# The mixer of a conv/delta-rule layer: heads' Gram chains side by side, inverse in batches, output rows in another order, finer turns, and a planner with other durations

## The chip, the cores and the metric

The kernel runs on 1 core of one Trainium2 chip. The metric is the device time of one execution in microseconds (us); several executions are given by their median. Engines are named as in the profile: PE (TensorE matmul), PEld (its weight load), DVE (VectorE), ACT (ScalarE), POOL (GpSimd), SP (SyncE, which issues the DMAs).

## The reference

One layer on x of 2048 x 1024, float32. The mixer, which the change touches, computes

```python
h = adaln(x, ...)
p = h @ w_in[layer]
gate_b, gate_c, h_conv, q, k, v, z, a, bt = jnp.split(p, split_at, axis=-1)
ya = gate_b * causal_depthwise_conv(gate_c * h_conv, conv_w_mix[layer])
ya = rms_norm(ya.reshape(b, s, CONV_GROUPS, CONV_GROUP_DIM), ...)
qkv = jax.nn.silu(causal_depthwise_conv(jnp.concatenate([q, k, v], axis=-1), conv_w_qkv[layer]))
...
o = chunked_gated_delta_rule(q, k, v, g_dec, beta)
o = rms_norm(o, g_dn_out[layer]) * jax.nn.silu(z)
y = jnp.concatenate([ya, yb], axis=-1) @ w_out[layer]
x = x + gate_m[:, None, :] * y
```

with 4 heads of 128; the delta rule solves one unit lower triangular system per head and chunk (`tri = I + beta * k k^T * decay`) and carries a 128 x 128 state per head from chunk to chunk. A feed-forward part (gate/up and down projections) and a last norm follow; the change leaves their code alone.

## The kernel before, in words

**Stages.** The mixer goes over 4 blocks (`b`) of 512 tokens, each of CH = 4 chunks of 128. Every dense product is done in float32r with high and low halves, three matmuls of 128x512 for one; all of them are issued by `dmm` (L302 to L306; the profile puts them at L304). In a block the dense stream on PE is: strips of the projection for k, q, v (4 heads each, 24 matmuls a strip), 3 strips of z, then for m = 0..3 three strips of the convolution part (`gate_c`, `h_conv`, `gate_b`), the fourth strip of z, and the output projection: 2 halves n of 4 row groups kp, each 24 matmuls over 4 chunk tiles t. kp 0 and 1 read `ya` (the convolution half, tiles yah and yal), kp 2 and 3 read `yb` (the delta-rule half, tiles ym). Block 0 runs part of its first strips before the turn of the mixer proper.

**Side chains.** The rest is written as generators that `spawn` puts on a list. After each Q = 6 dense matmuls `tick` resumes each generator whose awaited tiles are ready by the planner's reckoning (`due`), or which counts down a number of ticks:
- `head_chain`: the gates a, b are turned (L832), a series of some 25 small POOL operations gives g (L836 to L870), a cumulative sum on PE (L874 to L876), then decay masks `E` (POOL L885, PE L890, ACT L893, POOL L894). Then for one head after another the Gram chain: k is transposed (L812), squares are summed (ACT L818), `kd` and M = k k^T * E * bk are made (DVE L903, L913, POOL L905, L914), the 32x32 diagonal blocks are masked out (POOL L918) and gathered (DVE L922). Then the inverse of all diagonal blocks: out to DRAM and in again in another layout (L932, L937), 31 elimination steps on DVE (L946, L948), out and in again (L954, L956), and the block diagonal matrices X by 32 POOL operations of 128x64 (L965).
- `q_chain` (L1038, L1039), `v_chain` (L1053); `level_chain`, two heads in each: X transposed on DVE (L982), the mask M of the level on POOL (L984), then products and updates on PE, ACT and DVE (L990 to L1025).
- `chunk_chain`: for each of the 4 chunks the three hops PE L1075/L1078, DVE L1080 to L1083 -> PE L1087, DVE L1091 -> PE L1095/L1097, DVE L1103/L1104; POOL L1082 decays the state.
- `out_chain` per chunk: sums of squares (ACT L1112), scales (POOL L1113 to L1117), waits for all 4 strips of z (`yield from wait("z", NH)`), transposes (PE L1123), DVE L1125, ACT L1129 and DVE L1130 make the `yb` tiles ym.
- `mix_chain` per m: squares, group sums on PE (L1196, L1197), root, reciprocal (DVE L1200), yah and yal (L1202, L1203).
- `transpose_split`: the next block's x is turned (PE L528) and split (ACT L533, DVE L534, L535); `second_norm` turns the finished rows of the block before for the next stage (ACT L505, L554, PE L559).

**What sets the order.** `Clock` notes each instruction as it is emitted, with a modelled begin and end from a table of durations (`COST` and the branches of `note`). From the strips of q on (`clock.pinned`) each engine's instructions, and the DMA issues of SP, are pinned in the order of their modelled begins; nothing may overtake. Weights come through `next_w`, three strips ahead, in the order of `requests`, split by ACT L371 (high) and DVE L373 (low). PSUM has 4 banks pd for the dense stream and 4 banks pm for the chains. `drain` empties the list of chains; it stands ahead of the last tile of kp 2, n = 0, and at the block's end.

## Time and profile before

| | |
|---|---|
| median of 3 runs | 2571.94 us (2569.77 to 2575.55) |
| the profiled execution's own time | 2577.32 us |
| its span, first to last instruction | 2575.3 us |
| mean granted TensorE clock | 0.972 |
| busy: PE, DVE, ACT, POOL | 2388.1, 1839.5, 1014.1, 678.0 us |
| mixer blocks 0, 1, 2, 3, roughly | 62 to 337, 337 to 638, 638 to 934, 934 to 1227 us |
| gate/up products, down products | 1227 to 2098, 2098 to 2575 us |

Matmuls overlap in the records, so one of 128x512 lasts about 0.39 us while they follow each other every 0.23 us; a wait shows as idle time before an instruction and what ended it (`[2.17 <-ACT ym L1129]`). The granted clock is 1.0 or 0.5 at any one time, and a view by windows shows its mean.

### The profile page before, as it was taken

Reading aid. Unit: us, or ns where it says so; the run is one execution under the profiler, and the core shown is the slowest. Engines: PE = TensorE matmul, PEld = TensorE weight load, DVE = VectorE, ACT = ScalarE, POOL = GpSimd, SP = SyncE. Lnnn points to the kernel's source line nnn. Section 1 sums busy time; section 2 is a strip of 40 time slices with the busy share of each in tenths; the row PEclk is TensorE's granted clock in tenths of the full one; section 3 lists DMA queues with packets and bytes.
Section 4 is the critical chain, followed back from the end, with each engine's and each line's share of the span. In section 5 each row is a group of like instructions: output and inputs, shape, how many; then the busy total and the mean of one; then the engine's idle time right before and its main releaser. Section 6 shows DMA issues by size and latency. Waiting matters only on the chain. (4 is left out here: it accounts for less than half of the span.)

```text
span 2575.3 us, 30876 instructions
## 1 busy us (share of the span) xinstructions
PE 2388.1 (93%) x11243; PEld 1956.8 (76%) x11243; DVE 1839.5 (71%) x2594; ACT 1014.1 (39%) x1764; POOL 678.0 (26%) x800
## 2 busy tenths in 40 slices
PE   6879988899899999899799999999999999999996
PEld 4768777787677777787578888878888877887774
DVE  6886659866696657777766565787565559878898
ACT  3533445234543446234643333533333323322332
POOL 2631256113642236212100000000000036434426
PEclk9999999999999999999899999999999999999998
DMA  7442345524452344324575333564333265333332
GB/s 235 115 103 66 115 139 172 142 70 133 150 143 66 111 135 116 94 59 150 171 221 177 94 115 109 165 201 142 92 115 109 87 216 180 111 117 125 126 133 114
DMA packets 397534, 336.98 MB, mean 131 GB/s; under 512 B 39475, under 2 KB 338748, under 8 KB 397382
## 3 DMA queue, kind: packets, MB, share of 16 engines
q1 hardware_dynamic: 397126, 334.91, 42.4%
q8 instruction: 88, 1.44, 0.2%
q14 instruction: 64, 0.52, 0.1%
q10 hardware_dynamic: 256, 0.10, 0.0%
HBM read 261.55 MB, written 73.41 MB: 130 GB/s over the span
## 5 line engine op out<-in xcount | busy, mean ns | idle before, releaser
L371 ACT CAST whi<-wraw 128x1024 fp32r<-128x1024 f32 x278 | 291.9, 1050 | 388.5 <-PE pd L304 192.8
L373 DVE TENSOR_TENSOR wlo<-wraw,whi 128x1024 fp32r<-128x1024 f32 x275 | 341.2, 1242 | 108.1 <-ACT whi L371 105.4
L304 PE MATMUL pd<-hTh,whi 128*128 128x512 f32 x896 | 367.0, 410 | 1.1 <-DVE hTh L534 1.1
L304 PE MATMUL pd<-hTl,whi 128*128 128x512 f32 x896 | 355.9, 397 | 1.1 <-DVE hTl L535 1.1
L304 PE MATMUL pd<-hTh,wlo 128*128 128x512 f32 x896 | 355.4, 397 | 0.0
L1478 POOL TENSOR_TENSOR wraw<-wraw 128x1024 f32<-128x1024 f32 x2 | 5.0, 2522 | 786.5 <-DMA wraw<-in_w_down_dram 786.5
L304 PEld LDWEIGHTS pd<-hTh,whi 128*128 128x128 f32 x896 | 172.7, 193 | 37.2 <-DVE hTh L534 2.6
L304 PEld LDWEIGHTS pd<-hTh,wlo 128*128 128x128 f32 x896 | 171.9, 192 | 37.2
L304 PEld LDWEIGHTS pd<-hTl,whi 128*128 128x128 f32 x896 | 172.2, 192 | 35.8 <-DVE hTl L535 2.2
L1672 DVE TENSOR_TENSOR acc<-acc,pd 128x512 f32<-128x512 f32 x192 | 127.9, 679 | 29.6 <-PE pd L304 28.7
L1432 DVE TENSOR_TENSOR sg<-sg,pd 128x512 f32<-128x512 f32 x44 | 30.2, 687 | 165.6 <-PE pd L304 157.7
L1555 ACT CAST xh<-ra 128x640 fp32r<-128x640 f32 (+1 forms) x88 | 62.6, 719 | 197.8 <-PE pm L304 162.4
L1164 DVE SCALAR_TENSOR_TENSOR cv<-cb,pcb,cv 128x512 f32<-128x512 f32 x144 | 130.2, 904 | 4.6
L1564 POOL TENSOR_TENSOR xl<-ra,xh 128x640 fp32r<-128x640 f32 (+1 forms) x40 | 67.2, 1680 | 159.1 <-ACT xh L1555 154.8
L304 PE MATMUL pd<-whi,ym 128*128 128x512 f32 x256 | 93.7, 430 | 11.9 <-ACT ym L1129 11.9
L1672 DVE TENSOR_TENSOR acc<-acc,pm 128x512 f32<-128x512 f32 x120 | 81.6, 681 | 18.1 <-PE pm L304 17.6
L1272 POOL TENSOR_TENSOR cv<-cv 128x512 f32<-128x512 f32 x32 | 46.6, 1464 | 137.7 <-DVE cv L1271 93.2
L1601 POOL TENSOR_TENSOR wraw<-wraw 128x512 f32<-128x512 f32 x40 | 69.8, 1765 | 44.2 <-DMA wraw<-in_w_down_dram 44.2
L1082 POOL TENSOR_TENSOR state<-state,eg 128x512 f32<-128x512 f32 x15 | 21.2, 1411 | 225.8 <-PE pm L1078 225.7
L1200 DVE RECIPROCAL cv<-cv 128x512 f32<-128x512 f32 x16 | 53.7, 3353 | 35.6 <-ACT cv L1199 35.6
L965 POOL TENSOR_TENSOR X<-Dg,ck 128x64 f32<-128x64 f32 x128 | 40.0, 351 | 144.0 <-DMA Dg<-dx 144.0
L304 PE MATMUL pd<-S2h,whi 128*128 128x512 f32 x176 | 69.6, 395 | 7.3 <-ACT whi L371 7.3
(455 smaller groups left out, 6499.7 us busy)
## 6 DMA issues: line engine op xcount, KB each, us to landing
wraw<-in_w_in_dram SPq DMA_DIRECT2D x112, 512.0 KB, 4.4
wraw<-in_w_gate_up_dram SPq DMA_DIRECT2D x88, 512.0 KB, 3.9
ra<-act SPq DMA_DIRECT2D x80, 448.0 KB, 4.1
act<-S SPq DMA_DIRECT2D x80, 256.0 KB, 2.3
act<-act SPq DMA_DIRECT2D x68, 256.0 KB, 2.2
wraw<-in_w_ada_dram SPq DMA_DIRECT2D x32, 512.0 KB, 3.9
wraw<-in_w_out_dram SPq DMA_DIRECT2D x32, 512.0 KB, 3.7
wraw<-in_w_down_dram SPq DMA_DIRECT2D x22, 512.0 KB, 3.5
```

The costliest lines, as they stand in the source:

```text
L304: mm(*args, **kw)
L371: nc.scalar.copy(hi, raw)
L373: (lo_engines.popleft() if lo_engines else nc.vector).tensor_sub(lo, raw, hi.bitcast(F32))
L965: nc.gpsimd.tensor_mul(Xv[:, e, j], xc[:, e, h * CH + j].unsqueeze(1).to_broadcast([P, NBASE, HB]), bmb)
L1164: nc.vector.scalar_tensor_tensor(cv, cb[:, t:t + BLK], tap[t], cv, op0=ALU.mult, op1=ALU.add)
L1200: nc.vector.reciprocal(sy, sy)
L1272: nc.gpsimd.tensor_add(xr, xr, yo)
L1432: nc.vector.tensor_add(s5[i], s5[i], a[i])
L1555: nc.scalar.copy(hi, raw[:, c0:c1, :])
L1564: eng.tensor_sub(lo, raw, hi.bitcast(F32))
L1601: nc.gpsimd.tensor_mul(r[:, hs], r[:, hs], gate_f[:, hs])
L1672: nc.vector.tensor_add(accs[s, u][:, ns], accs[s, u][:, ns], ps)
```

## The change

- **Planner.** Other durations: POOL operations cost 0.14 us and 1.7 ns an element, and 0.42 or 0.6 us more while DVE is busy by the plan; a hand-over between engines 0.2 us (was 0.15); on one engine 0.1 us (0.14 on POOL, 0 on PE), where nothing was charged. A chain may ask `due` for two free pm banks (`yield 2, ...`), and one of lower standing for one more.
- **Turns.** In the mixer `tick` runs after each 3 dense matmuls; head, diagonal, level, chunk and out chains are asked first.
- **Gram chains.** Masking and gathering of the diagonal blocks and the level's mask M (before: in `level_chain`) go into a `diagonal_chain` per head, so that the next head's Gram product need not wait for it.
- **Inverse.** The elimination steps are emitted four at a time, each batch by a time of the plan. X is made by 8 operations of 128x256, those of heads 2 and 3 on DVE.
- **Dense order.** All 4 strips of z come before the convolution part. The output's row groups run kp 0, 2, 3, 1 in each half. `drain` ahead of the last tile of kp 2 stays in the last block alone.

```diff
+KPS = 0, 2, 3, 1
...
+    AGAIN = {"EngineType.PE": 0.0, "EngineType.Pool": 0.14}
...
-                cost = 0.2 + n * 2.0e-3
+                cost = 0.14 + n * 1.7e-3 + (0.42 if n < 200 else 0.6) * self.busy("EngineType.DVE", start)
...
+    FIRST_CHAINS = "head_chain", "diagonal_chain", "level_chain", "chunk_chain", "out_chain"
+
     def spawn(gen, delay=1):
-        side.append([gen, delay])
+        side.append([gen, delay, gen.__name__ not in FIRST_CHAINS])
+        side.sort(key=lambda e: e[2])
...
-    def due(w):
-        return max([clock.next_free("pm"), *(clock.ready(t) for t in w)]) + 0.3
+    def due(w, low):
+        banks, w = (w[0], w[1:]) if isinstance(w[0], int) else (1, w)
+        return max([clock.next_free("pm", banks + low), *(clock.ready(t) for t in w)]) + 0.3
...
-        if count[0] % Q == 0:
+        if count[0] % (Q // 2 if mixing[0] else Q) == 0:
...
-                    yield kT[:, h, :],
+                    yield 2, kT[:, h, :]
...
-                    yield from take("lv", 1)
-                    md = lv_tile([P, CH, NBASE, BASE])
...
                     done["kk"] += 1
-                    yield md,
-                    nc.vector.tensor_reduce(Dg[:, h], md.rearrange("p j b c -> p j c b"), op=ALU.add, axis=AX.X)
-                    give("lv", 1)
+                    spawn(diagonal_chain(M, Dg[:, h]), 1)
                 nc.gpsimd.tensor_mul(sk, sk, nk)
                 done["sk"] = True
-                yield 1
+                yield from wait("dg", NH)
...
-                    if k % 2:
-                        yield mxq,
+                    if k % 4 == 1:
+                        yield clock.ready(mxq, True) - 1.5
...
-                    for j in range(CH):
-                        for e in range(2):
-                            nc.gpsimd.tensor_mul(Xv[:, e, j], xc[:, e, h * CH + j].unsqueeze(1).to_broadcast([P, NBASE, HB]), bmb)
+                    for e in range(2):
+                        (nc.vector if h > 1 else nc.gpsimd).tensor_mul(
+                            Xv[:, e], xc[:, e, h * CH:(h + 1) * CH].unsqueeze(2).to_broadcast([P, CH, NBASE, HB]), by_base(HB))
...
+            def diagonal_chain(M, dst):
+                yield from take("lv", 1)
+                md = lv_tile([P, CH, NBASE, BASE])
+                nc.gpsimd.tensor_mul(md, M.rearrange("p j (b c) -> p j b c", c=BASE), by_base(BASE))
+                yield md,
+                nc.vector.tensor_reduce(dst, md.rearrange("p j b c -> p j c b"), op=ALU.add, axis=AX.X)
+                give("lv", 1)
+                mm_ = ap_.tile([P, CH, P], F32, name="ym", bufs=8)
+                nc.gpsimd.tensor_mul(mm_, M, bm(lmask[LEVELS[0]], CH))
+                Mms.append(mm_)
+                done["dg"] += 1
...
-            for h in range(NH - 1):
-                z_strip(h)
...
-            z_strip(NH - 1)
...
-                for kp in range(4):
+                for kp in KPS:
...
                         if n == 0 and kp == 2 and t == CH - 1:
-                            drain()
                             if b + 1 < NB:
                                 spawn(transpose_split(xblock(b + 1), Gm, Sm, *hT), 1)
                             else:
+                                drain()
                                 clock.pinned = mixing[0] = False
...
-                            dmm(pso[t], yl, wh[:, k, :], start=False, stop=(kp == 3 and k == 1))
+                            dmm(pso[t], yl, wh[:, k, :], start=False, stop=(kp == KPS[-1] and k == 1))
```

What this does to the order is shown at three places of block 1 (the changed kernel's lines are 6 to 13 higher for the same code: L914 becomes L920, L1123 becomes L1135).

POOL, the Gram chains of the first heads (sk, ym, lv: scale, M and masked M of a head; nq, rq: of q; ss: the finished rows' norm), before:

```order
L905 TENSOR_TENSOR sk_2769<-nk_2767,mhalf_86 128x4
L914 TENSOR_TENSOR ym_3214<-ym_3214,bk_2770 128x512
L918 TENSOR_TENSOR lv_3217<-ym_3214,ck_80 128x512
L1040 TENSOR_SCALAR nq_2768<-nq_2768 128x4
L1041 TENSOR_TENSOR rq_2771<-nq_2768,mhalf_86 128x4
L1042 TENSOR_SCALAR rq_2771<-rq_2771 128x4
L499 TENSOR_SCALAR ss_3176<-ss_3176 128x1
L500 TENSOR_TENSOR ss_3176<-ss_3176,mhalf_86 128x1
L905 TENSOR_TENSOR sk_2769<-nk_2767,mhalf_86 128x4
L914 TENSOR_TENSOR ym_3333<-ym_3333,bk_2770 128x512
L918 TENSOR_TENSOR lv_3336<-ym_3333,ck_80 128x512
```

And now:

```order
L911 TENSOR_TENSOR sk_2745<-nk_2743,mhalf_86 128x4
L920 TENSOR_TENSOR ym_3269<-ym_3269,bk_2746 128x512
L911 TENSOR_TENSOR sk_2745<-nk_2743,mhalf_86 128x4
L920 TENSOR_TENSOR ym_3294<-ym_3294,bk_2746 128x512
L1047 TENSOR_TENSOR lv_3297<-ym_3269,ck_80 128x512
L1047 TENSOR_TENSOR lv_3302<-ym_3294,ck_80 128x512
L911 TENSOR_TENSOR sk_2745<-nk_2743,mhalf_86 128x4
L505 TENSOR_SCALAR ss_3187<-ss_3187 128x1
L506 TENSOR_TENSOR ss_3187<-ss_3187,mhalf_86 128x1
L920 TENSOR_TENSOR ym_3332<-ym_3332,bk_2746 128x512
L911 TENSOR_TENSOR sk_2745<-nk_2743,mhalf_86 128x4
L924 TENSOR_TENSOR sk_2745<-sk_2745,nk_2743 128x16
```

Two heads' M stand side by side, their masks (now L1047) follow, and the operations on q (L1040 to L1042 before) are behind all four heads.

DVE, the end of the inverse (yal: the matrices in elimination; X: the block diagonal ones; cb, cv: convolution part; wlo: low halves of weights), before:

```order
L948 TENSOR_TENSOR yal<-yal,lv 128x16
L1220 TENSOR_TENSOR cb<-pd,cv 128x512
L1222 COPY uhalo_2759<-cb 128x2
L1225 TENSOR_SCALAR cv<-cb,pcb 128x512
L1227 SCALAR_TENSOR_TENSOR cv<-cb,pcb,cv 128x512 x2
L373 TENSOR_TENSOR wlo<-wraw,whi 128x1024
L438 SCALAR_TENSOR_TENSOR wraw<-wraw,cs 128x1024
L1219 COPY cb<-uhalo_512 128x2
L1231 TENSOR_TENSOR cv<-cv,pd 128x512
L982 STREAM_TRANSPOSE lv<-X 128x512
```

And now:

```order
L948 TENSOR_TENSOR yal<-yal,lv 128x16
L1241 TENSOR_TENSOR cv<-cv,pd 128x512
L380 TENSOR_TENSOR wlo<-wraw,whi 128x1024
L1203 TENSOR_TENSOR lv<-cv,lv 128x512
L380 TENSOR_TENSOR wlo<-wraw,whi 128x1024
L1210 RECIPROCAL cv<-cv 128x512
L463 TENSOR_TENSOR Sf<-pd,pca 128x8
L1211 SCALAR_TENSOR_TENSOR cv<-cv,pcb 128x512
L963 TENSOR_TENSOR X<-Dg,ck 128x256 x2
L1213 TENSOR_TENSOR yal<-cv,yah 128x512
L963 TENSOR_TENSOR X<-Dg,ck 128x256 x2
L981 STREAM_TRANSPOSE lv<-X 128x512 x4
```

Between the last elimination step and the transposes of X stand now the first mix chain's subtraction, reciprocal and product (L1193, L1200, L1201 before), which stood behind the transposes; the convolution's L1220 to L1227 of the first m went ahead of the last steps.

PE, the last chunk's products and the turning of its output (kd, E, ch: chunk chain; ck,ch: the transposes of `out_chain`; ym and yah: output projection; hT: projection), before:

```order
L1095 MATMUL pm<-ch,kd 128x128 x4
L1097 MATMUL pm<-ch,E 128x128 x4
L1123 MATMUL pm<-ck,ch 128x128 x4
L304 MATMUL pd<-whi,ym 128x512
L304 MATMUL pd<-wlo,ym 128x512
```

And now the turning of the last chunk's output (the products L1107 and L1109 of that chunk are 39 dense matmuls ahead of it):

```order
L311 MATMUL pd<-hTh,wlo 128x512
L1135 MATMUL pm<-ck,ch 128x128 x4
L311 MATMUL pd<-hTh,whi 128x512
L311 MATMUL pd<-hTl,whi 128x512
L311 MATMUL pd<-hTh,wlo 128x512
L311 MATMUL pd<-whi,yah 128x512
L311 MATMUL pd<-wlo,yah 128x512
```

The last chunk was worked among matmuls that read ym; now its output is turned while the projection still runs.

The places of the steps on PE, as the number of dense matmuls of the block that stand ahead of them (counted in the order; 864 in a block, `yb` is read from number 720 on before and from 696 on now; in block 0 the count starts 60 matmuls into the block, so there 660 and 636):

| step | block 0 | block 1 | block 2 | block 3 |
|---|---|---|---|---|
| L832, before -> now | 12 -> 6 | 30 -> 36 | 30 -> 36 | 30 -> 36 |
| L874 (g) | 60 -> 51 | 96 -> 114 | 96 -> 114 | 90 -> 114 |
| L911, four heads | 96, 138, 180, 204 -> 120, 141, 165, 192 | 138, 174, 216, 246 -> 177, 180, 192, 195 | 138, 174, 216, 246 -> 177, 180, 192, 195 | 144, 180, 210, 234 -> 189, 198, 207, 225 |
| L990 (X needed) | 372 -> 429 | 492 -> 528 | 432, 444 -> 489 | 414, 432 -> 444 |
| L1075 of the last chunk | 660 -> 537 | 720 -> 609 | 720 -> 600 | 720 -> 537 |
| L1123, last | 678 -> 585 | 738 -> 669 | 738 -> 663 | 749 -> 597 |
| L528, first (next block's x) | 690 -> 660 | 750 -> 720 | 750 -> 720 | - |

More of the change, by code (lines that the diff above doesn't have):

```diff
@@ L77, in fit, with busy @@
         return s + cost
+    def busy(self, name, t):
+        return not any(a <= t < b for a, b in self.gaps[name])
     @staticmethod
@@ L91, in ready @@
         a, b, c, d = self.box(ap)
-        return max([0.0] + [t + (0.15 if x != eng else 0.0) for (e, f, g, h), w, t, x in self.touched[ap.name]
+        return max([0.0] + [t + (0.2 if x != eng else self.AGAIN.get(eng, 0.1)) for (e, f, g, h), w, t, x in self.touched[ap.name]
                             if (w or write) and a < f and e < b and c < h and g < d])
@@ L114, in place, with next_free @@
         return self.free_at[tensor.name]
-    def next_free(self, name):
+    def next_free(self, name, n):
         tag = next((t for t in self.slots if t.startswith(name + "_")), None)
         row = [x for x in self.slots[tag] if x not in self.kept] if tag else []
-        return self.used[row[0]] if len(row) >= 4 else 0.0
-    def next_free(self, name):
-        tag = next((t for t in self.slots if t.startswith(name + "_")), None)
-        row = self.slots[tag] if tag else []
-        return self.used[row[-4]] if len(row) >= 4 else 0.0
+        return max(self.used[x] for x in row[:n]) if len(row) >= 4 else 0.0
     def note(self, i):
@@ L138, in note @@
             begin = self.fit(eng, start, 0.45) - 0.45
-            end = self.fit("DMA", begin + 1.0, cost) + 0.6
+            end = self.fit("DMA", begin + 1.2, cost) + 0.8
             self.order(eng, begin, i)
@@ L285, in tick @@
                 go = e[1] <= 0
+            elif isinstance(e[1], float):
+                go = e[1] <= clock.pe
             else:
-                go = due(e[1]) <= clock.pe
+                go = due(e[1], e[2]) <= clock.pe
             if go:
@@ L294, in tick @@
                     ran = True
-        times = [due(e[1]) for e in side if not isinstance(e[1], int)]
+        times = [e[1] if isinstance(e[1], float) else due(e[1], e[2]) for e in side if not isinstance(e[1], int)]
         if must and not ran and times:
@@ L388, in requests @@
             for c0 in (2048, 1536, 2560, 3072):
-                for h in range(NH - (c0 == 3072)):
+                for h in range(NH):
                     yield col_strip, w_in, c0 + h * P
@@ L445, in settled @@
         yield
-        while clock.pinned and due(tiles) > clock.pe:
+        while clock.pinned and due(tiles, 0) > clock.pe:
             yield
@@ L1001, in level_chain @@
                 T, Y = {}, {}
-                yield tuple(Xs[h] for h in hs)
+                yield 2, *(Xs[h] for h in hs)
                 yield from take("lv", len(hs))
@@ L1239, in layer_kernel @@
                 pso = [dense_ps() for _ in range(CH)]
-                for kp in range(4):
+                for kp in KPS:
                     wh, wl = next_w()
```

39 lines of the change are left out of this document (18 added, 21 removed).

## The prediction

> **What bounds the kernel now.** The windows by stage came first: the stretch of the four mixer blocks, one block of it, and the first 73 us behind the mixer.
>
> ```profile
> core 0: us, PE busy (x) PEld busy (x) DVE busy (x) ACT busy (x) POOL busy (x), PEclk, DMA share, GB/s
> 62.00:1227.00 1165.00, 1062.29 (x5510) 878.80 (x5508) 845.25 (x1304) 503.42 (x1017) 423.40 (x601) 0.96 0.40 116
> 337.00:638.00 301.00, 272.98 (x1436) 225.93 (x1435) 220.78 (x337) 128.15 (x256) 111.91 (x156) 0.95 0.44 131
> 1227.00:1300.00 73.00, 58.72 (x250) 45.24 (x249) 47.18 (x63) 47.00 (x69) 8.14 (x11) 0.88 0.56 173
> ```
>
> PE is the busiest engine, yet it stands idle for 1165.0 - 1062.3 = 102.7 us of the mixer, and its granted clock there is 0.96 and not 1. DVE, next, is busy for 220.8 of block 1's 301 us, so the block is not DVE's as a whole. What can be won is PE's idle time and its lost clock. PE's own waits in the mixer say for whom:
>
> ```profile
> PE pm L874 <- POOL g L863: 26.3, 4, 7.8
> PE pm L990 <- DVE lv L982: 18.1, 4, 5.9
> PE pd L304 <- ACT ym L1129: 11.9, 6, 2.2
> PE pm L559 <- ACT wraw L554: 11.2, 8, 2.8
> PE pm L812 <- ACT cv L1165: 8.8, 7, 2.0
> PE pm L1123 <- POOL ch L1117: 8.3, 4, 3.1
> PE pm L1197 <- DVE lv L1193: 6.1, 1, 6.1
> PE pm L479 <- DVE E L1039: 4.5, 1, 4.5
> PE pm L1196 <- ACT lv L1192: 1.8, 1, 1.8
> ```
>
> Columns are total us, times, longest. These nine hold 97.0 of the 102.7 us. I call them A (the gate g, 26.3), B (the inverse: 18.1, and the 6.1 and 1.8 of a mix chain whose DVE step stands behind the inverse's, 26.0 together), C (the last outputs, 11.9 + 8.3 = 20.2), and the rest: L559, L812 and L479. The chain that ended last covers only the kernel's tail and says nothing here. The price of a matmul's place in the stream is that chain's row of six:
>
> ```profile
> 2352.01 1.36 PE pm L304 x6
> ```
>
> so 0.2267 us each. How many stand between two steps comes from the order; how long a step takes, from the trace.
>
> **A, the gate.** PE in block 1, and POOL, where the chain from L832 to L874 runs:
>
> ```profile
> 349.77 0.42 PE L832 MATMUL pm<-ck,cv 16*128 16x16 f32 x4
> 373.06 0.61 PE L874 MATMUL pm<-g,ck 128*128 128x16 f32 x2 [6.27 <-POOL g L863]
> ...
> 359.95 0.96 POOL L848 TENSOR_SCALAR sp_s<-sp_e 128x16 f32<-128x16 f32 x1 [3.73 <-ACT sp_e L845]
> 368.40 1.08 POOL L856 TENSOR_TENSOR sp_p<-sp_p,sp_z 128x16 f32<-128x16 f32 x1
> 369.90 0.22 POOL L856 TENSOR_TENSOR sp_p<-sp_p,sp_z 128x16 f32<-128x16 f32 x1
> ```
>
> The chain takes 23 us, 10 of them until ACT's exponential and 13 on POOL; the change takes nothing out of it. What covers it changes: 66 dense matmuls stood between, 78 stand now in blocks 1 and 2 (12 x 0.2267 = 2.7 us each), 78 for 60 in block 3 (4.1), 45 for 48 in block 0 (-0.7). Sum: -8.8 us, and 17.5 of the 26.3 stay. Bounds: one more copy stands ahead of the exponential on ACT, and POOL's 13 us hang on what else runs (one operation takes 1.08 us or 0.22, the two rows of L856); I take the count, and 3 us either way as an estimate.
>
> **B, the inverse.** POOL, DVE and PE in block 1:
>
> ```profile
> 489.96 9.79 POOL L965 TENSOR_TENSOR X<-Dg,ck 128x64 f32<-128x64 f32 x31 [0.97 <-DMA Dg<-dx]
> ...
> 491.80 0.71 DVE L982 STREAM_TRANSPOSE lv<-X 128x512 f32<-128x512 f32 x1 [4.32 <-POOL X L965]
> 501.39 0.65 DVE L1193 TENSOR_TENSOR lv<-cv,lv 128x512 fp32r<-128x512 f32 x1
> ...
> 502.09 0.79 PE L1197 MATMUL pm<-lv,gones_r 128*128 128x512 f32 x1 [6.12 <-DVE lv L1193]
> ```
>
> X takes 9.8 us on POOL after its data has landed; DVE waits for it, and a mix chain's L1193 stands behind in DVE's queue, for which PE waits in turn. Now X is 8 operations of 128x256, four on POOL, four on DVE. No row has that shape: on POOL it lies between 0.32 (9.79 / 31) and 1.47 (the page's L984, 128x512),
>
> ```profile
> L984 POOL TENSOR_TENSOR ym<-ym,ck 128x512 f32<-128x512 f32 x16 | 23.0, 1468 | 0.2
> ```
>
> by size 0.81, so four take 3.2 us; on DVE under 0.71 (L982, 128x512), by size 0.36, four 1.4. X is then ready 6.6 us sooner. The two rows of L856 show that a POOL operation can take 0.22 us or 1.08. [...] Against the sum speaks the order on DVE: the elimination ends one convolution step later than before (L1220 to L1227, and now L1231, stand around it). But L990 too stands later on PE, by 57, 36, 45 or 57, and 30 matmuls, 6.8 us or more, where B's waits were 26.0 / 4 = 6.5 us a block, and L1193 now stands ahead of X. I leave 1.5 us a block: -20. Bounds: -26, and -10 if half the shift is eaten by the later end.
>
> **C, the last outputs.** PE in block 1, then the first square and the last scaling of the next block's x on ACT:
>
> ```profile
> 596.07 0.60 PE L1123 MATMUL pm<-ck,ch 128*128 128x128 f32 x4
> 598.84 0.50 PE L304 MATMUL pd<-whi,ym 128*128 128x512 f32 x1 [2.17 <-ACT ym L1129]
> 605.38 0.79 PE L304 MATMUL pd<-whi,ym 128*128 128x512 f32 x1 [1.49 <-ACT ym L1129]
> ...
> 593.54 1.06 ACT L505 ACTIVATE ht<-kq 128x1024 bf16<-128x1024 f32 x1 [2.86 <-DMA kq<-in_x_dram]
> 605.23 2.18 ACT L521 ACTIVATE kq<-kq,ss 128x1024 f32<-128x1024 f32 x2
> ```
>
> Here the turned output is needed 6 matmuls after it is turned. With all z strips ahead of the convolution part the chains need not stop after chunk 1: the last L1123 stands at 585, 669, 663 and 597, the first `yb` matmul at 696 (636 in block 0). The shortest cover is 27 matmuls, 6.1 us, for a chain of 2.8 us (596.07 to 598.84). kp 0 ahead, kp 1 last cover the last mix chains. The next block's x can load once the last chunk has read k and q, over 100 matmuls (23 us) ahead of its turning, where the chain from 593.54 to 607.41 takes 14. So all of C goes: -20.2.
>
> **The rest.** L479's one wait, in block 0, is for what DVE does around L1039; it now stands ahead of the first L1038 and 24 matmuls farther on: -2 (0 to -4.5). L559 and L812 wait for ACT and DVE work that is not shortened: 0 (-10 to +10). Moving the level's mask to the diagonal chains, the finer turns (switches between the two kinds of matmul go from 372 to 386, by the order) and DVE's 1.4 us of X: covered by idle POOL and DVE, within the term for new waits below.
>
> **The clock.** Windows on three waits of A, B and C:
>
> ```profile
> 373.00:377.00 4.00, 3.94 (x12) 3.43 (x13) 0.65 (x3) 1.72 (x4) 3.85 (x7) 0.50 0.02 7
> 502.00:507.00 5.00, 4.91 (x16) 4.24 (x17) 4.89 (x9) 0.69 (x1) 0.00 (x0) 0.50 0.39 104
> 600.00:609.00 9.00, 6.38 (x17) 4.25 (x17) 1.44 (x2) 6.91 (x11) 4.67 (x10) 0.50 0.00 1
> ```
>
> After each kind of wait PE runs at half clock. The mixer loses 0.04 x 1165 = 46.6 us so; in these windows PE works 15.2 of 18 us, so 39 us cost matmuls. Of A, B and C (72.5 us) 23.5 stay, 68% go: 27 us; since a short wait can cost a whole half-clock stretch, I take -22 (-12 to -27).
>
> **Behind the mixer** PE waits for the feed-forward's first sums:
>
> ```profile
> PE pd L304 <- ACT whi L371: 7.3, 1, 7.3
> PE pd L304 <- ACT A11h L574: 3.4, 1, 3.4
> PE pd L304 <- DVE A11l L575: 0.9, 1, 0.9
> ```
>
> They start at the last tile of kp 2, now 24 matmuls earlier: -5.4 of 11.6 (0 to -8).
>
> **New waits.** All four chunks now run beside the convolution part; 24 of their hops (two chunks, three hops, four blocks) are new there. A hop's DVE step can stand behind another operation:
>
> ```profile
> L373 DVE TENSOR_TENSOR wlo<-wraw,whi 128x1024 fp32r<-128x1024 f32 x275 | 341.2, 1242 | 108.1 <-ACT whi L371 105.4
> PE pm L1087 <- DVE ch L1081: 0.4, 1, 0.4
> ```
>
> The chunks already there waited 0.4 us in all (second row), one L373 in front costs 1.24: 0 to +30, I take half a microsecond a hop, +12.
>
> **Sum**: -8.8 - 20 - 20.2 - 2 - 22 - 5.4 + 12 = -66. The profiled execution's own time of 2577.3 becomes 2511; the median of the runs lies 5.4 below it, at 2571.9, so 2506.
>
> **The rivals.**
> 1. DVE becomes the bound of the stretch behind the inverse.
>
> ```profile
> 500.00:613.00 113.00, 106.01 (x624) 90.44 (x625) 74.82 (x94) 44.32 (x91) 22.53 (x36) 0.92 0.28 84
> 390.00:490.00 100.00, 91.29 (x465) 75.74 (x464) 92.94 (x175) 41.67 (x106) 39.01 (x40) 1.00 0.58 162
> ...
> L535 DVE TENSOR_TENSOR hTl<-ht,hTh 128x512 fp32r<-128x512 f32 x32 | 32.8, 1027 | 1.0
> ```
>
> DVE has 75 us of work in block 1's stretch, and gets 7 more pairs of L534 and L535 (7 x 1.03 for the second, 10 for both as an estimate), less three L373 (3.7): 81. PE's own work in the new stretch is 240 x 0.2267 = 54, and some 220 small matmuls of the chains at 0.11 to 0.15 (L1123's four in 0.60): 79 to 87. At 93% (DVE's share from 390 to 490 us, second row) 81 takes 87.5, up to 8.5 us a block more than PE: +34, 2540. For it: those loads; against it: DVE was idle for a third of this stretch.
> 2. The inverse's end moves as far as L990 does. B and its part of the clock (26/72.5 of 22) stay: +28, 2534. For it: the elimination is emitted in longer batches and still stands among the same L373; against it: X's 6.6 us.
> 3. Slower: the serial chunk chain among DVE's long operations. 47 hops (16 chunks; block 0's first chunk has two), each behind one L373 and one operation like L1193 (0.65) would cost 47 x 1.89 = 89 against gains of 78: +11, 2583. It decides from 78 / 47 = 1.7 us a hop. Against it: the 0.4 us above.
> 4. Short waits cost no clock. If half clock follows only single waits of several microseconds, as in A and B, then C (28% of the 39 us, 11) gives back nothing there, and the clock term is 22/27 of that, 9, smaller: 2515. The window at 600 us speaks against it: its waits are 2.2 us or less, its clock 0.50. [...]
>
> **How the numbers follow.** Chances: the forecast 0.58, rival 1 0.15, rival 2 0.12, rival 3 0.09, rival 4 0.06. The likeliest's own range takes all of B (-6), L479 (-2.5), no new wait (-12), more clock (-5), more behind the mixer (-2.6) and half of the rest's -10: 2506 - 33 = 2473; I go on to 2465 for the whole -10 with A's 3. Upward B -10 (+10), new waits +30 (+18), clock -12 (+10), nothing behind the mixer (+5.4): 2549, which takes in rivals 1, 2 and 4; 2552 with A's 3. Left out is rival 3. A measurement of this kernel tells apart about 0.2%, 5 us. Faster: 0.58 + 0.15 + 0.12 + 0.06, less 0.03 for cases between rivals 1 and 3: 0.88; within 0.2% 0.03; slower 0.09.
>
> **What would show it.** A: L874's waits at 17 to 18 us. B: L990, L1196 and L1197 under 7 together, POOL's L963 near 0.8 each. C: no wait for L1129's counterpart. The clock of the mixer's window at 0.98. Rival 1 shows as dense matmuls and chains that wait for DVE while DVE has no idle time; rival 2 as L981 behind L963 late on DVE; rival 3 as waits of L1087's and L1095's counterparts of over 1.7 us. The prediction is wrong if the mixer doesn't get some 60 us shorter, or if the time changes outside it.

## The result and the profile after

The changed kernel takes 2485.57 us (median of 4 runs, 2484.74 to 2487.72) where the kernel before takes 2571.98 (4 runs, 2569.77 to 2575.55): a ratio of 0.9664, 95% interval 0.9647 to 0.9681, or 86.4 us less. The forecast was 2506, its range 2465 to 2552. The profiled execution of the changed kernel has an own time of 2487.72 and a span of 2485.9 us, 89.6 and 89.4 less than the profiled execution before.

First the stages. The two windows are the mixer (from block 0's first L838, L832 before, to the first up product of the feed-forward) and the first 76 us behind it:

```profile
core 0: us, PE busy (x) PEld busy (x) DVE busy (x) ACT busy (x) POOL busy (x), PEclk, DMA share, GB/s
62.20:1146.80 1084.60, 1033.28 (x5488) 859.54 (x5488) 851.38 (x1335) 518.10 (x1032) 391.86 (x489) 0.98 0.43 124
1146.80:1222.80 76.00, 70.82 (x314) 57.70 (x313) 45.17 (x60) 46.38 (x64) 7.52 (x11) 0.96 0.60 187
```

The same mixer before, from its first L832 to its first up product, took 1158.7 us, with PE busy for 1055.99. So it is 74.1 us shorter: PE idle fell from 102.7 to 51.3 (-51.4), and PE's busy time, from 1056.0 to 1033.3 (-22.7). That is the clock, 0.96 then and 0.98 now: the window even holds 6 dense matmuls more, since L838 stands 6 places earlier in block 0 than L832 did. Of the other 15.3 us of the span 12.2 lie behind the mixer (1351.3 to 1339.1), most of it in the first 76 us, where PE's idle time was 14.3 and is 5.2. The last 3.1 lie ahead of it (65.3 to 62.2): 1.4 of them are those 6 matmuls, which now count as the mixer's, and the rest I take for scatter, since the runs below have 62.0 to 65.5 there.

PE's waits (total us, times, longest) answer to those shown of before:

```profile
PE pm L880 <- POOL g L869: 20.1, 4, 8.6
PE pd L311 <- ACT whi L378: 4.9, 2, 4.7
PE pd L311 <- DVE cv L1280: 4.8, 3, 2.5
PE pm L818 <- DVE E L1036: 4.6, 2, 4.1
PE pm L565 <- ACT wraw L560: 3.6, 1, 3.6
PE pm L896 <- POOL lv L891: 2.9, 2, 1.5
PE pm L818 <- DVE cb L1169: 2.6, 2, 2.4
PE pm L1135 <- POOL ch L1129: 2.2, 4, 0.9
PE pm L485 <- DVE wraw L480: 2.0, 1, 2.0
PE pm L1099 <- DVE ch L1093: 1.1, 2, 0.5
PE pm L987 <- DVE lv L981: 0.7, 1, 0.7
PE pm L1107 <- DVE ch L1103: 0.7, 1, 0.7
```

A (L880) fell only from 26.3 to 20.1. B's three rows are down to L987's 0.7; L1206 and L1207 wait for nobody. Of C's two rows one is left, L1135, with 2.2. The chunks' hops, L1099 and L1107, wait 1.8 us in all.

### The profile page after: what moved, and what is told of

The parts are those of the page before. It is cut to its first block, busy times and chain, and to the rows that moved or that the text cites. A ratio compares the mean times of both kernels' runs of the same rounds, so it can differ in the third digit from the quotient of the medians.

```text
span 2485.9 us, 30764 instructions
## 1 busy us (share of the span) xinstructions
PE 2356.5 (95%) x11243; PEld 1937.9 (78%) x11243; DVE 1833.5 (74%) x2610; ACT 1024.0 (41%) x1771; POOL 644.7 (26%) x688
## 5 line engine op out<-in xcount | busy, mean ns | idle before, releaser
L380 DVE TENSOR_TENSOR wlo<-wraw,whi 128x1024 fp32r<-128x1024 f32 x275 | 346.4, 1260 | 98.0 <-ACT whi L378 91.3
L1176 DVE SCALAR_TENSOR_TENSOR cv<-cb,pcb,cv 128x512 f32<-128x512 f32 x144 | 136.4, 947 | 3.7
L1681 DVE TENSOR_TENSOR acc<-acc,pm 128x512 f32<-128x512 f32 x120 | 81.5, 679 | 17.2 <-PE pm L311 16.8
L311 PE MATMUL pd<-whi,ym 128*128 128x512 f32 x256 | 86.5, 398 | 0.0
L311 PE MATMUL pd<-A22h,whi 128*128 128x512 f32 x176 | 69.1, 392 | 4.6 <-DVE sg L1441 4.6
L311 PE MATMUL pm<-S4h,whi 128*128 128x512 f32 x176 | 69.2, 393 | 2.7 <-ACT sg L1435 2.7
L311 PE MATMUL pd<-S2h,wlo 128*128 128x512 f32 x176 | 69.6, 395 | 0.5 <-DVE wlo L380 0.5
```

The costliest lines, as they stand in the source:

```text
L311: mm(*args, **kw)
L380: (lo_engines.popleft() if lo_engines else nc.vector).tensor_sub(lo, raw, hi.bitcast(F32))
L1176: nc.vector.scalar_tensor_tensor(cv, cb[:, t:t + BLK], tap[t], cv, op0=ALU.mult, op1=ALU.add)
L1681: nc.vector.tensor_add(accs[s, u][:, ns], accs[s, u][:, ns], ps)
```

## The experiments

The theory to test, T: three places waited (A, B, C), the change takes the waits of B and C and part of A's away by new shapes and new places, and each us of wait costs some 0.4 us of clock besides. The rivals: the planner's new durations alone do it and the new structure does not matter; or one part of the structure does it. The diagonal chains, the longer batches of the elimination and the new rules of `due` and `spawn` are in no run undone by themselves. Most kernels here take one part back, or do one alone; each is compared with the kernel before on the same chip, so ratios are what to compare (0.9664 for the changed kernel). "Idle" and "busy" are PE's in the mixer, in the same window of each profile. The expectations count places in dense matmuls from L838 on, which stands at 6 in block 0 and 36 in the others: L987's 528 of block 1 is 492 there.

| kernel | median us | ratio to before, 95% | mixer | idle | busy |
|---|---|---|---|---|---|
| before | 2571.98 | 1 | 1158.7 | 102.7 | 1056.0 |
| changed | 2485.57 | 0.9664 (0.9647 to 0.9681) | 1084.6 | 51.3 | 1033.3 |
| old_durations | 2562.94 | 0.9944 (0.9927 to 0.9962) | 1160.0 | 100.4 | 1059.6 |
| durations_alone | 2537.52 | 0.9861 (0.9841 to 0.9882) | 1124.9 | 74.7 | 1050.2 |
| pool_old_price | 2494.37 | 0.9693 (0.9672 to 0.9714) | 1093.7 | 52.2 | 1041.5 |
| x_in_32 | 2497.32 | 0.9686 (0.9669 to 0.9704) | 1093.9 | 56.0 | 1037.9 |
| old_outputs | 2532.00 | 0.9825 (0.9807 to 0.9844) | 1121.1 | 70.7 | 1050.4 |
| kp_in_order | 2530.26 | 0.9816 (0.9799 to 0.9833) | 1134.1 | 81.4 | 1052.7 |
| z_strip_last | 2555.50 | 0.9916 (0.9900 to 0.9933) | 1142.4 | 85.5 | 1056.9 |
| turns_of_6 | 2514.48 | 0.9756 (0.9738 to 0.9774) | 1117.2 | 69.2 | 1048.0 |
| turns_of_2 | 2487.46 | 0.9665 (0.9644 to 0.9686) | 1092.7 | 52.3 | 1040.4 |
| gate_price | 2484.75 | 0.9662 (0.9635 to 0.9688) | 1085.1 | 44.8 | 1040.3 |
| gate_alone | 2484.32 | 0.9636 (0.9619 to 0.9653) | 1080.0 | 46.2 | 1033.8 |
| gate_by_log | 2477.65 | 0.9627 (0.9614 to 0.9640) | 1078.5 | 42.4 | 1036.1 |

### The durations: old_durations, durations_alone, pool_old_price

```diff
-    return max([0.0] + [t + (0.2 if x != eng else self.AGAIN.get(eng, 0.1)) ...
+    return max([0.0] + [t + (0.15 if x != eng else 0.0) ...
-    cost = 0.14 + n * 1.7e-3 + (0.42 if n < 200 else 0.6) * self.busy("EngineType.DVE", start)
+    cost = 0.2 + n * 2.0e-3
...
```

> The changed kernel with the planner's old durations (hand-over 0.15 us, POOL 0.2 us + 2 ns an element whatever DVE does, the old DVE, ACT and DMA prices); X, masks, output order and turns stay changed. In the order the gate's matmul L880 then stands 36, 39, 39 and 39 dense matmuls behind L838 instead of 45, 78, 78 and 78, the first level product L987 at 333 to 381 instead of 408 to 492. Theory 1, the gain hangs on where the durations put the chains: L880 waits 8.8 us more in blocks 1 to 3 and 2 us more in block 0 (+28), the level products stand 20 to 60 matmuls earlier than A's added wait makes good (+5 us a block, +20), and each us of wait costs 0.4 us of clock: 2486 + 48 x 1.4 = 2553, L880's waits near 48 us. Rival, the gain is in the new structure (X in 8 operations, order of the outputs) and any placement will do: waits only move, under +15, so below 2501.

0.9944: 2.8% of the time come back, some 72 us, and the mixer's 1160.0 us are those of the kernel before. So with the old durations the new structure wins nothing in the mixer. The rival falls. But the working of theory 1 was wrong too. The waits:

```profile
PE pm L880 <- POOL g L869: 22.7, 4, 10.5
PE pm L818 <- ACT cv L1177: 20.9, 8, 8.1
PE pm L565 <- ACT wraw L560: 11.3, 5, 3.7
PE pm L987 <- DVE lv L981: 9.9, 3, 4.3
PE pm L1135 <- POOL ch L1129: 7.4, 10, 1.7
```

A is 22.7 and not 48. What came back are the heads' and the next x's turns (L818 and L565, 32.2 us in these rows) and part of B and C: PE reaches step after step before its data. Next the other way about, the new durations in the kernel before:

> The kernel before with the planner's new durations alone (prices, hand-over, POOL's surcharge while DVE is busy); X, masks, output order, turns and rules of the kernel before. In the order the gate stands at 54, 72, 72 and 72 instead of 48, 66, 66 and 60 dense matmuls; the first level product at 570, 606, 534 and 540 instead of 360, 462, 402 and 384, and in blocks 0 and 1 all four chunks within 30 to 40 matmuls of the first output matmul at 648 and 684. Theory 1, durations and structure need each other: A gets 1.4 us a block less (-6), B's 26 us go, but four chunks of four hops of some 2 us stand within 9 us in blocks 0 and 1 (25 us of wait each) and C's 20 us stay: +18 of waits and 0.5 us of clock for each us, 2572 + 27 = 2599. Rival, the durations alone carry the gain: A and B go as in the changed kernel, 2572 - 32 x 1.4 = 2527.

0.9861, some 36 us of the 86, so neither theory's figure: above the rival's 2527, far under theory 1's 2599. In this kernel the lines are those of before plus 4:

```profile
PE pm L878 <- POOL g L867: 20.1, 4, 6.4
PE pd L308 <- ACT ym L1133: 18.2, 10, 2.2
PE pm L1127 <- POOL ch L1121: 8.3, 4, 3.1
PE pm L563 <- ACT wraw L558: 4.6, 5, 1.9
```

No wait for the inverse is left: **B goes by the planner's durations, with X still in 32 operations.** L559's counterpart fell from 11.2 to 4.6. C's two rows stay and grow, 26.5 for 20.2, since in this order the chunks all come late. The serial chunks that I had priced at 25 us a block wait 5.1 us in all.

One price alone:

> The changed kernel with POOL's old price alone in the planner (0.2 us + 2 ns an element, no surcharge while DVE is busy). The gate stands at 51, 57, 57 and 57 instead of 45, 78, 78 and 78; the levels at 423, 540, 453 and 405, as in the changed kernel but for block 1. Theory 1, this one price places the gate: L880's waits grow by 4.8 us in blocks 1 to 3 and shrink by 1.4 in block 0, 33 us in all for 20, with 6 of clock, 2486 + 19 = 2505; B stays away, since the chains behind the gate stand where they stood. Rival, the hand-over of 0.2 us and the DVE prices carry the old_durations loss: within 6 us of 2486.

0.9693, no difference that the intervals can tell from 0.9664. So POOL's price, taken back alone, costs little of old_durations' 72 us. The hand-over, the gap on one engine and the prices of DVE, ACT and DMA stay new here, and no run takes these apart. L880's wait did not grow to 33 us but fell to 12.1, with the gate 21 matmuls nearer in three blocks. Block 1's chain shows why; PE, then ACT, in this kernel:

```profile
333.56 0.42 PE L838 MATMUL pm<-ck,cv 16*128 16x16 f32 x4
349.62 0.40 PE L880 MATMUL pm<-g,ck 128*128 128x16 f32 x2 [1.52 <-POOL g L869]
...
335.89 0.22 ACT L851 ACTIVATE sp_e<-sp_n 128x16 f32<-128x16 f32 x1
```

and in the changed kernel:

```profile
330.38 0.42 PE L838 MATMUL pm<-ck,cv 16*128 16x16 f32 x4
353.45 0.61 PE L880 MATMUL pm<-g,ck 128*128 128x16 f32 x2 [3.77 <-POOL g L869]
...
340.44 0.22 ACT L851 ACTIVATE sp_e<-sp_n 128x16 f32<-128x16 f32 x1
```

The exponential starts 10.1 us behind L838 in the changed kernel and 2.3 here. So how long the chain takes hangs on ACT's order. With the exponential 2.3 to 4.4 us behind L838 it took 14 to 18 us in blocks 1 to 3 of this kernel and of old_durations, for 23 with it 10 us behind. That is not all of it: in block 0 of the changed kernel the exponential starts 2.9 us behind L838 and the chain still takes 19.5 us, 16 of them on POOL.

### B: x_in_32

```diff
-  for e in range(2):
-      (nc.vector if h > 1 else nc.gpsimd).tensor_mul(Xv[:, e], ..., by_base(HB))
+  for j in range(CH):
+      for e in range(2):
+          nc.gpsimd.tensor_mul(Xv[:, e, j], ..., bmb)
```

> The changed kernel with X made as before by 32 operations of 128x64 on POOL alone; the mask stays with the diagonal chains. The planner knows the longer way and puts L987 at 444 or 459, 489 or 513, 477 and 456 instead of 423, 492, 453 and 408 dense matmuls. Theory 1 (term B as predicted: X 6.6 us sooner is what removes the waits): waits of 5 us a block come back at the level products, +20 with 8 of clock, 2514. Rival, the waits went because the planner now knows how long X takes and puts the products behind it: L987's line waits under 3 us in all, the chunks only move back, and the time stays within 8 us of 2486.

0.9686 against 0.9664, intervals that overlap: some 6 us by the medians. No row of the inverse's product is among this kernel's waits. So the rival holds in its result: the planner puts the products behind the inverse, whichever way X is made. With durations_alone this shows from both sides that it is not X's new shape that removes B.

The rival's reason, that the planner now knows how long X takes, does not hold as it stands. The old price of one of X's 32 operations is 0.2 + 64 x 0.002 = 0.33 us, and it took 0.32 (9.79 / 31); with POOL's old price alone (pool_old_price) L987 waits only 0.9 us. What the old durations had too short is the elimination. Two of its steps, each of which needs the one ahead of it, on DVE in block 1 before:

```profile
470.06 0.29 DVE L946 TENSOR_TENSOR lv<-yal 128x130 f32<-128x130 f32 x1
470.39 0.29 DVE L948 TENSOR_TENSOR yal<-yal,lv 128x130 f32<-128x130 f32 x1
```

One starts 0.33 us behind the other. The old durations count 0.22 for it (0.08 + 130 x 0.00105, and nothing between two on one engine), the new ones 0.33 (0.09 instead of 0.08, and 0.1 between the two). Over the 62 operations of a block that is some 7 us, as an estimate, where B's waits were 6.5. That it is this entry that moved the products was not run by itself; the hand-over and the DMA prices rose too.

### C: old_outputs, kp_in_order, z_strip_last

```diff
-KPS = 0, 2, 3, 1
+KPS = 0, 1, 2, 3
```

is kp_in_order. z_strip_last puts the last z strip and its request behind the convolution part. old_outputs does both and has the drain in every block.

> The changed kernel with the last outputs as before: one z strip behind the convolution part, kp in the order 0, 1, 2, 3, the drain ahead of the last tile of kp 2. The last two outputs are again turned 6 to 9 matmuls ahead of their use. Theory 1 (term C): the waits of the dense matmul for L1129's counterpart and of L1135 come back, 18 us, with 7 us of clock, and the feed-forward's first sums start 24 matmuls later (+5): 2486 + 30 = 2516. Rival, with the planner's new durations the chunks run early enough anyway: C's waits stay under 6 us in all and the time within 8 us of the changed kernel, 2486 to 2494.

0.9825, some 41 us, more than theory 1's 30. Its lines stand up to one later than in the changed kernel:

```profile
PE pm L819 <- DVE E L1037: 15.6, 5, 7.5
PE pd L311 <- ACT A11h L581: 8.5, 1, 8.5
PE pd L311 <- ACT ym L1142: 8.4, 6, 1.9
PE pd L311 <- ACT whi L378: 7.3, 1, 7.3
PE pm L1136 <- POOL ch L1130: 5.4, 4, 1.4
```

The last outputs wait 13.8 us again (2.2 in the changed kernel), the feed-forward's first sums 15.8 (some 5), as expected; L819's 11 more I had not foreseen, nor L918's 6.1 for DVE (0.5 in the changed kernel). Then the two edits apart:

> The changed kernel with the output's kp in the order 0, 1, 2, 3 alone; the z strips stay ahead, no drain. All chains stand where they stood; the first yb matmul moves 24 matmuls later, to 654 and 684, behind last turns at 579 and 633, while the first kp 1 matmul moves 48 earlier, to 630 and 660, behind the last mix chain's product L1206 at 624 and 657. Theory 1, the new kp order serves the mix chains: behind L1206 stand the root on ACT, L1210's 3.4 us and L1211 to L1213 on DVE, some 7 us, for a cover of 0.7 us in blocks 1 to 3: 6 us of wait a block there and 5 in block 0, less what the other order now waits, 20 us and 9 of clock: 2515. Rival, the kp order carries nothing, since the last turns stand 27 matmuls and more ahead in either order: within 6 us of 2486.

0.9816, some 39 us: theory 1, with a higher price. The chains stand where they stood, and these rows grow:

```profile
PE pd L311 <- DVE cv L1280: 16.6, 8, 2.6
PE pd L311 <- ACT yah L1212: 16.2, 4, 4.5
```

The second is the wait for the last mix chain, four times of up to 4.5 us, which the changed kernel does not have. The first, 4.8 there, is the wait for a PSUM bank that the first half's scaling (L1280, on DVE) still reads. In block 1 DVE splits the next block's x (L540, L541) until 598.6 us and scales only then, while PE is through with the half at 596.7. The turning of that x is let go at the last tile of kp 2, which in this order stands 24 matmuls nearer to the half's end.

> The changed kernel with one z strip behind the convolution part again, kp order and drain as changed. The last three outputs are turned at 612, 642, 648 in block 0 and 642 to 680, 672 to 695 in the others, for a first use at 630 and 660; two of four chunks stand within 30 matmuls ahead of it. Theory 1, what the z strips ahead bring is room for the chunks: L1135 and the matmul behind L1129's counterpart wait 4 to 5 us a block again, 18 us and 9 of clock, 2513. Rival, the room is not needed, since kp 1 is now last and covers the last outputs' turns: within 6 us of 2486.

0.9916, some 65 us, worse than both edits undone together:

```profile
PE pd L311 <- ACT ym L1142: 12.6, 7, 2.3
PE pm L1136 <- POOL ch L1130: 5.3, 4, 2.0
PE pm L1108 <- DVE ch L1104: 3.8, 7, 0.8
PE pm L1100 <- DVE ch L1094: 2.3, 4, 0.7
```

The last outputs and hops wait 24 us. L819 and L918 wait 15.2 and 5.9 us for DVE here too, against 4.6 and 0.5 in kp_in_order, so these waits go with the z strip's place and not with the kp order. Neither half of C is worth anything alone: against the changed kernel the one with the z strips ahead and the old kp order (kp_in_order) loses 39 us, the one with the new kp order and the z strip behind 65, the one with both as before 41. The z strips ahead leave the mix chains without cover, the new kp order needs the outputs 24 matmuls sooner, and each makes room for the other.

### The turns: turns_of_6, turns_of_2

```diff
-        if count[0] % (Q // 2 if mixing[0] else Q) == 0:
+        if count[0] % Q == 0:
```

> The changed kernel with the chains' turns every 6 dense matmuls as before, in place of every 3 in the mixer. The gate stays at 78 in blocks 1 to 3 (54 for 45 in block 0: 2 us less wait), most other steps come 3 to 60 matmuls later. Theory 1 (turns cost nothing in themselves): within 8 us of 2486, with the sign open; in block 1 the chunks' last outputs are turned at 678 for a first use at 660, up to 4 us of wait for L1135 and what follows. Rival, the finer turns carry a part of the gain, since a step that is due waits 1.5 matmuls less: 100 steps a block of which the serial chain holds some 40, 40 x 1.5 x 0.2267 = 14 us a block that the serial chain ends later; where it is the bound, in the last third of a block, PE waits for 5 us more a block: 2506.

0.9756, some 24 us: the rival, and my term for this edit (nothing) was wrong.

```profile
PE pm L818 <- ACT cv L1177: 16.1, 6, 3.7
PE pd L311 <- DVE cv L1280: 14.1, 9, 4.2
PE pm L1135 <- POOL ch L1129: 7.4, 3, 5.4
```

L1135 is the late end of a block, as expected of levels that stand up to 48 matmuls later; L1280 stands at the change of the output's halves, and why it grows here is not shown. That the heads' turns (L818) wait 16.1 us for the activation, 0.5 with turns of 3, was not expected, and I have no tested reason for it. Finer still:

> The changed kernel with the chains' turns every 2 dense matmuls in the mixer instead of every 3. Placements shift by 1 to 30 matmuls, mostly ahead. Theory 1, what the finer turns bring is a shorter lag of each due step (turns of 6 for 3 cost 29 us, 1.5 matmuls of mean lag): 0.5 matmul of lag, -10, 2476. Rival, the gain of turns of 3 came from one placement (block 1's last outputs at 678 with turns of 6, 633 with turns of 3), which turns of 2 (632) leave as it is: within 5 us of 2486; more switches between the two kinds of matmul would then show as up to +5.

0.9665: no change. The gain ends at 3, as the rival had it.

### A: gate_price, gate_alone, gate_by_log

A is the largest wait that is left. gate_price and gate_alone mend the planner's estimate (a price of one kind of operation), gate_by_log shortens the chain itself.

> The changed kernel with one price changed: a small POOL operation (under 200 elements) costs the planner at least 0.27 us more, whether DVE's work of that time is noted yet or not. The chain of the gate is planned as a whole ahead of DVE's later work, so the surcharge for a busy DVE misses it: planned 0.31 us from one such operation to the next, while the trace has 0.6 to 0.8 in blocks 0 and 1. The gate stands at 75, 87, 87 and 84 instead of 45, 78, 78 and 78. Theory 1 (A's rest is the planner's short estimate, one matmul more of cover is 0.227 us less of wait): 8.6 - 6.8, 3.8 - 2.0, 3.6 - 2.0 and 4.1 - 1.4 = 7.9 us for 20.1, with 0.44 us of clock for each us: -17, 2469; block 1's last outputs now stand at 678 with a first use at 660, up to +5. Rival, the wait moves on to L896, whose two POOL products of 1 to 2 us stand just behind the gate: under 6 us gained, 2480 to 2492.

L880's wait fell from 20.1 to 3.3 us, one wait in block 0, more than expected, and the time did not move: 0.9662. L896 stays at 2.9, so the wait did not move there. What grew is dense matmuls that wait for `wlo`, 2.0 to 8.2, L1135, 2.2 to 4.7, and 7 us of PE's busy time. But this price moved the levels too, so:

```diff
-    cost = 0.14 + n * 1.7e-3 + (0.42 if n < 200 else 0.6) * self.busy("EngineType.DVE", start)
+    cost = 0.14 + n * 1.7e-3 + max(self.more, (0.42 if n < 200 else 0.6) * self.busy("EngineType.DVE", start))
```

with `self.more` at 0.12 between L838 and the gate, else 0.

> The changed kernel with 0.12 us more for each POOL operation of the gate's chain alone, in the planner's estimate. The gate stands at 60, 90, 90 and 90 instead of 45, 78, 78 and 78 dense matmuls, the first level product at 423, 495, 453 and 408 as in the changed kernel (492 in block 1). So A is changed with nearly nothing else. Theory 1, A's wait is time of the program: 15 and 12 matmuls of cover are 3.4 and 3 x 2.7 us less of wait, 8.5 of 20.1 stay, with 0.44 us of clock for each us: -17, 2469. Rival 1, the wait moves on to L896, behind whose POOL products it then stands: L896 takes what L880 gives, 2484 to 2488. Rival 2, an earlier wait only lets DVE, ACT and the loads catch up: L880's waits go, and later waits (L311 for wlo, L818, L1135) grow by as much, 2480 to 2488.

```profile
PE pm L820 <- ACT cv L1181: 11.4, 4, 4.8
PE pm L884 <- POOL g L872: 9.4, 4, 6.7
```

The gate (now L884) waits 9.4 us, as worked out (8.5), and the heads' turns behind it (L820) wait 11.4 for the activation instead of 0.5, and 14.2 instead of 7.7 for all engines. That is rival 2. The ratio, 0.9636, is a little lower, with an interval that overlaps the changed kernel's.

Last, the chain. ACT's Ln stands in for the series; the gate's values are then not the series' values, so this kernel gives a time and is no version to use.

```diff
-    nc.gpsimd.tensor_scalar_add(sg, ex[:, 0], 2.0)
...
-    nc.gpsimd.tensor_mul(pl, pl, sg)
+    nc.scalar.activation(pl, ex[:, 0], AF.Ln, bias=ones[:, 0:1])
```

> The changed kernel with the gate's logarithm taken by one ACT operation (Ln of the exponential plus 1) instead of the series: 19 of the 22 small POOL operations between the exponential and g go, as does DVE's reciprocal there, and ACT gets a table load more. The gate stands at 21, 54, 54 and 54 instead of 45, 78, 78 and 78, the levels at 465, 492, 453 and 405 instead of 423, 492, 453 and 408. The chain is then 10 us to the exponential, some 1.5 us for load and logarithm and 1 us on POOL, 12.5 us (block 0: 6), for a cover of 12.2 us (4.8). Theory 1 (a wait of the program that is taken away is time won, with 0.44 us of clock): L880 waits under 5 us in all for 20.1, and POOL is busy 40 us less: 2486 - 15 x 1.44 = 2464. Rival (the gate's wait is slack for what stands behind it, as gate_alone showed: ACT's and DVE's later work then makes PE wait): L818 and the dense matmuls' waits grow by what L880's lose, 2478 to 2488.

```profile
PE pd L311 <- DVE wlo L380: 6.1, 4, 2.3
PE pm L485 <- DVE wraw L480: 4.7, 2, 2.4
PE pm L818 <- ACT cv L1166: 2.9, 1, 2.9
```

L880's wait is gone altogether, POOL is busy 37 us less in the mixer, and the time falls by 0.4% (0.9627, under the changed kernel's interval): 9 us, between theory 1's 22 and the rival's 8 or less. PE's idle time falls by 8.9 where A was 20.1: over half of it turns up at steps behind, at other engines. The two runs before agree: L880 loses 16.8 in gate_price and 10.7 in gate_alone, PE's idle time 6.5 and 5.1. More than half of A was time in which DVE, ACT and the loads caught up.

## Why the prediction was right, and where its terms were off

Against the profiled execution, in us:

| term | forecast | measured | from |
|---|---|---|---|
| A | -8.8 | -6.2 | 26.3 to 20.1 |
| B | -20 | -25.3 | 26.0 to 0.7 |
| C | -20.2 | -18.0 | 20.2 to 2.2 |
| L479 (now L485) | -2 | -2.5 | 4.5 to 2.0 |
| L559, L812 | 0 | -12.8 | 24.1 to 11.3, all releasers |
| new waits | +12 | +13.5 | the other rows of the mixer |
| clock in the mixer | -22 | -22.7 | PE's busy time |
| behind the mixer | -5.4 | -12.2 | 1351.3 to 1339.1 |
| ahead of it | 0 | -3.1 | the window's start, scatter |
| sum | -66 | -89.3 | |

**Right**: the stage, the three places, the sign and rough size of each, and the clock, which came within 1 us. Of its signs of being wrong one shows in part: the mixer got 74 us shorter, as asked, but the time outside it changed too, by 15.3 us where the sum itself has 5.4. **The two terms that were off** make 20 of the missing 23 us. "L559 and L812 wait for ACT and DVE work that is not shortened: 0" asked what gets shorter and not what gets placed better: old_durations brings these waits back (L818 20.9 for the activation alone, L565 11.3), durations_alone halves L559's. And behind the mixer I counted 24 matmuls of earlier start, 5.4 us, where PE's idle time fell by 9.1 (14.3 to 5.2) and its clock there rose from 0.89 to 0.96. With the drain and the old output order back in old_outputs the stage behind the mixer takes 1347.8 us, against 1339.1; durations_alone, which has both as well, takes 1340.0. So how much of the 12.2 us the earlier start brings stays open.

**A.** The count of matmuls held in three blocks: block 0's wait went from 7.8 to 8.6 (+0.7 forecast), those of blocks 1 and 2 from 6.3 to 3.8 and 3.6 (-2.7 each). Block 3's went from 5.9 to 4.1, where the count gave -4.1: its chain grew from 22.2 to 23.4 us. That "the change takes nothing out of" the chain's 23 us was true by luck: the planner also sets when ACT takes the exponential, and other placements have 14 to 18 us.

**B.** Right in its result, wrong in its first reason, so the size came out by luck. I let X's 6.6 us carry the term, but making X as before costs some 6 us of time and brings no wait for the inverse back. What carries it is the later place of L990, which I named second; the new durations bring it, and the elimination is where the old ones were too short. Rival 2 (the end moves as far as L990) is refuted by L987's 0.7.

**C.** Its working held: outputs turned early, kp 1 as cover for the mix chains. What I had not seen is that neither half works alone.

**The turns** I counted at nothing "within the term for new waits"; taking them back costs some 24 us. The costs of taking single parts back (durations 72, outputs 41, turns 24, X 6) come to 143 where the whole won 86: the parts need each other, and none has a share of its own.

**New waits and rivals 1 and 3.** The term's size was right, its makeup not: the chunks' hops wait 1.8 us and not 12, so rival 3 falls. The 13.5 us are at the output's banks (L1280 4.8), L896 (2.9) and single rows. Rival 1 falls: in its stretch of block 1, from 480 to 600 us, DVE is busy for 85.5 of the 120 us, as the rival had it, and PE idle for only 0.7; in the whole mixer DVE is busy 851 of 1085 us (840 of 1159 before) and PE's waits for it are short. It is the engine that the next gain meets, though: in gate_by_log six of PE's eight largest waits of the mixer are for DVE.

**The clock and rival 4.** Over the fourteen kernels of the table PE's busy time in the mixer rises by 0.42 us for each us of idle time, within 6 us of a straight line; old_outputs and kp_in_order, whose added waits are 4.5 us and less for the most part, lose as much clock as the long waits of before or more (17.1 us for 19.4 of idle time, 19.5 for 30.0, against 22.7 for 51.4). So short waits do cost clock, and rival 4 falls.

## What to carry to other kernels

Where a planner sets the order, ask of each wait what the planner believed the chain to take, and measure that duration where it runs, beside the other engines' work; a part that is rightly priced needs no shortening. Take parts of a change back one at a time before crediting any: here the single parts' costs add up to more than the whole won, and the one that looked the best reason (X) was worth little. A wait that goes is time won only if the steps behind it are ready; look at what they wait for next before you spend work on the longest row.

## What the runs showed of the hardware

A small POOL operation beside a busy DVE. In the gate's chain of the changed kernel, block 1, in order of time:

```profile
346.61 1.08 POOL L862 TENSOR_TENSOR sp_p<-sp_p,sp_z 128x16 f32<-128x16 f32 x1
...
350.94 0.22 POOL L862 TENSOR_TENSOR sp_p<-sp_p,sp_z 128x16 f32<-128x16 f32 x1
```

DVE works until 350.6 and idles then; the same operation takes 0.65 to 1.08 us ahead of that and 0.22 behind it. The planner's surcharge asks whether DVE is busy by what has been noted so far, and this chain is noted as a whole ahead of DVE's later work, so it is planned at 0.31 us from one operation to the next. X on both engines tells the same. L963 as a whole (least, median, longest in ns), then block 3's POOL and DVE:

```profile
L963 POOL TENSOR_TENSOR X<-Dg,ck x16: 612/792/1592, 190.5 to 1008.5; 128x256 f32<-128x256 f32 x16
L963 DVE TENSOR_TENSOR X<-Dg,ck x16: 415/424/842, 191.9 to 1008.0; 128x256 f32<-128x256 f32 x16
...
1006.93 2.36 POOL L963 TENSOR_TENSOR X<-Dg,ck 128x256 f32<-128x256 f32 x3 [0.70 <-DMA Dg<-dx]
...
1006.88 1.94 DVE L963 TENSOR_TENSOR X<-Dg,ck 128x256 f32<-128x256 f32 x3 [1.13 <-DMA Dg<-dx]
```

Three and three side by side take 2.41 us (1006.88 to 1009.29), where by the least durations POOL's three alone would take 1.84 and one engine behind the other 3.08. The measured time lies between the two; why is not shown.

The clock behind waits is no plain matter of their length. Windows of the changed kernel on one wait of 3.8 us, one of 3.6, and a group of 2.5 and less:

```profile
349.00:358.00 9.00, 5.23 (x17) 4.09 (x17) 1.57 (x3) 3.02 (x5) 7.81 (x19) 0.67 0.24 84
956.00:966.00 10.00, 6.40 (x37) 5.14 (x36) 9.86 (x15) 5.01 (x7) 9.58 (x10) 1.00 0.09 21
1114.00:1132.00 18.00, 13.18 (x57) 9.94 (x56) 16.13 (x24) 11.76 (x19) 5.92 (x4) 1.00 0.65 204
```

The first is followed by half clock (0.67 as the mean of its window), the second and third are not (1.00), while the group of 2.2 us and less in the prediction was (0.50). What decides it is not shown. Over a whole mixer the 0.42 us a us is the figure to use here.
